# Gates and u of a spatial-gating layer by seven block products instead of eight, multiplied onto y in place

## The chip, the cores and the metric

One core of one Trainium2 chip runs the kernel. Every time is the device time of one execution in microseconds (us). TensorE (PE) multiplies; it has a queue of its own for loading weight blocks (PEld). VectorE (DVE) and ScalarE (ACT) do the elementwise work, GpSimd (POOL) and SyncE (SP) issue transfers here.

## What is computed

Two layers on x of 512 rows by 1024 columns, in float32: differential attention, then causal spatial gating. The change is in the second layer, of branch width 2048:

```python
proj = h @ w_in                                  # 512x1024 @ 1024x6144
u = proj[..., :BRANCH]
v = rms_norm(proj[..., BRANCH:2 * BRANCH], v_gain)
gate = proj[..., 2 * BRANCH:]
y = jnp.einsum('gts,bcsgd->bctgd', w, v) + b_s   # w: causal 128x128 per group of 128 channels
return u * y * jax.nn.silu(gate)
```

The result goes through an output projection of 2048x1024, a residual sum and a last norm.

## The kernel before

**Exact products from two parts.** Each float32 operand is split into a high part (ACT rounds it to fp32r) and a low part (DVE subtracts), and a product takes three matmuls: high x high, high x low, low x high. h lies transposed in `hT[0]` and `hT[1]`, as 8 blocks of 128 channels by 512 rows.

**Weights by chunks.** `chunks` lists loads of 1 MB each. `Chunk(i)` (L140) splits chunk i in four pieces with `split` (L122: ACT L137, DVE L138), loads the two after it, and its `tick` splits the next chunk's pieces while PE works. Raw halves rotate through three buffers (`wraw`), split ones through three pairs (`wsp`).

**v by seven block products.** v's weights (1024x2048) are taken as two blocks of 1024x1024. `Quads` (L308) loads the four quarters a, b, c, d of a block (512x512 each), combines them (subtractions on DVE, L334; additions by an accumulating DMA on POOL's queue, L339), and splits each of seven forms (L347, L348). `sides` (L766) holds the seven matching forms of h: quarters of `hT`, and the sums s1 to s4 in a pool of their own, filled by `raw_sums` (L737). `product_n` (L768) gives one product: 2 row blocks x 4 channel blocks x 3 matmuls of 512 columns, 24 in all, with a block of h as the weights. The loop at L806 runs 2 blocks x 7 products. Beside product i it splits the form of product i + 2 (`beside`, `quads.work`). Two pairs of banks, px and py, collect the products; after some of them a state is kept on ACT (`keep`, L792) or added to a kept one on DVE (`plus`, L800), so that seven products give all four quarters of the block. v stands transposed in `yT`, in channel groups; `total` (L795) gathers its squares.

**Norm, then gates and u by chunks.** L858 to L862 make v's scale and multiply `yT` by it. w_s is loaded by POOL (L867), masked (L868) and transposed on PE (L889, L890). Then for each of 8 chunk pairs `gate(c)` projects two groups of gate channels with `proj_t` (L252: per group 8 channel blocks x 3 matmuls, a 128x128 block of weights against 512 columns of h) and applies Silu on ACT (L882). The loop at L891 mixes a group of v with w_s (L897, four matmuls into psy), adds gain and bias (L901), multiplies by the gate (L904), projects u (psu) and multiplies by it (L907), in place in `yT`.

**Output.** `out_half` (L278) splits `yT` into `hT`'s place and multiplies by the output's weights.

**What sets the order.** The program is written as one sequence. A planner (the tile framework) then orders each engine's instructions: among those that are ready by its own estimate of times, the earliest in the program goes first. It inserts the waits, too. Each engine then runs its list strictly in order, so that a wait holds up what stands behind it. `tc.issue_after` ties an instruction behind another by hand. Transfers of weights are issued on SyncE's queue, the accumulating ones and those of w_s and the bias on POOL's.

## Time and profile before

| what | value |
|---|---|
| median of 3 runs | 939.6 us (939.35 to 939.84) |
| profiled execution, its own time | 937.86 us |
| span of its instructions | 936.2 us |
| mean granted clock of TensorE | 0.998 of 2.4 GHz |

The span is the time from the first to the last instruction of the profiled execution; the rest of its own time lies around it. An engine's busy time is the time in which at least one of its instructions runs. A matmul's duration includes its way through the array, and matmuls overlap, so the distance between the starts of two neighbours is what one costs when they follow each other. A view of groups gives, per line of code and shape, the count, busy time, mean time of one, and the idle time ahead of it with what ended it.

### The profile page before, as it was taken

What the parts mean: (1) busy time and instruction counts of PE and PEld (TensorE: products, weight loads), DVE (VectorE), ACT (ScalarE), POOL (GpSimd) and SP (SyncE); (2) the same over time, 40 slices, a digit from 0 to 9 for tenths busy, and PEclk for the clock granted to TensorE, in tenths of its full rate; (3) what the DMA queues carried; (4) which work ended last, traced back from release to release, by engine and by line L of the source; (5) the groups of instructions that cost most, each with busy time, mean ns of one, the idle gap of its engine ahead of it and who ended that gap; (6) DMA issues with size and microseconds to landing.
All of it is one profiled execution on the core that took longest, in us unless ns stands there. A gap on an engine that the chain in (4) does not pass through costs nothing.

```text
span 936.2 us, 12287 instructions
## 1 busy us (share of the span) xinstructions
PE 918.1 (98%) x4553; PEld 751.9 (80%) x4553; DVE 539.4 (58%) x1329; ACT 414.5 (44%) x981; POOL 16.7 (2%) x29
## 2 busy tenths in 40 slices
PE   7999999999999999999999999999999999999996
PEld 5878887878787878787778887788888888888884
DVE  7532225757675667576877739955633333365634
ACT  6332334545454545555656426856322222233432
POOL 0000000000000000000000000001000000000000
PEclk9999999999999999999999999999999999999999
DMA  7432223222222223131214624545422222232202
GB/s 247 145 115 90 90 90 100 71 84 84 80 81 77 87 72 95 63 102 57 67 50 161 207 62 78 176 90 168 125 90 89 88 86 88 90 101 97 91 16 90
DMA packets 64795, 92.29 MB, mean 99 GB/s; under 512 B 3597, under 2 KB 44606, under 8 KB 64096
## 3 DMA queue, kind: packets, MB, share of 16 engines
q1 hardware_dynamic: 61408, 79.70, 26.5%
q0 software_dynamic: 2272, 10.49, 4.4%
q10 hardware_dynamic: 1056, 1.32, 0.5%
q8 instruction: 36, 0.59, 0.2%
q14 instruction: 23, 0.19, 0.1%
HBM read 85.17 MB, written 2.14 MB: 93 GB/s over the span
## 4 chain that ended last, share of the span: by engine, by line
PE 86%; DVE 8%; ACT 3%; DMA 1%; issue 1%; SPq 0%; ACTq 0%
PE psv L426 10%; PE psqk L256 6%; PE psqk L258 6%; PE psqk L257 6%; PE acc L293 5%; PE acc L291 5%; PE acc L292 5%; PE pss L565 3%; PE psg L256 3%; PE psu L257 3%; PE psu L256 3%; PE psu L258 3%; PE psg L257 3%; PE psgt L257 3%; PE psgt L256 3%; PE psg L258 3%
## 5 line engine op out<-in xcount | busy, mean ns | idle before, releaser
L138 DVE TENSOR_TENSOR lo<-raw,hi 128x512 fp32r<-128x512 f32 x256 | 165.1, 684 | 165.7 <-ACT hi L137 165.7
L137 ACT CAST hi<-raw 128x512 fp32r<-128x512 f32 x256 | 144.9, 618 | 208.5 <-PE psu L257 72.4
L256 PE MATMUL psqk<-hT,hi 128*128 128x512 f32 x256 | 104.3, 407 | 0.0
L578 ACT ACTIVATE e<-e,nm 128x384 f32<-128x384 f32 (+3 forms) x128 | 70.6, 553 | 67.5 <-DVE nm L575 67.5
L258 PE MATMUL psqk<-hT,lo 128*128 128x512 f32 x256 | 100.2, 391 | 0.0
L257 PE MATMUL psqk<-hT,hi 128*128 128x512 f32 x256 | 99.9, 390 | 0.0
L291 PE MATMUL acc<-hi,hT 128*128 128x512 f32 x224 | 88.1, 393 | 0.0
L293 PE MATMUL acc<-hi,hT 128*128 128x512 f32 x224 | 87.4, 390 | 0.0
L292 PE MATMUL acc<-lo,hT 128*128 128x512 f32 x224 | 87.3, 390 | 0.0
L426 PE MATMUL psv<-hi,hT 128*128 128x512 f32 x256 | 86.8, 405 | 0.5 <-ACT hT L247 0.5
L575 DVE CUSTOM_DVE_ANT_0 e<-pss,bias 128x384 f32<-128x384 f32 (+3 forms) x128 | 55.6, 485 | 17.6 <-PE pss L565 17.4
L426 PEld LDWEIGHTS psv<-hi,hT 128*128 128x128 f32 x256 | 48.6, 190 | 13.9 <-issue 2.2
L256 PEld LDWEIGHTS psqk<-hT,hi 128*128 128x128 f32 x256 | 48.1, 188 | 12.9 <-issue 2.6
L258 PEld LDWEIGHTS psqk<-hT,lo 128*128 128x128 f32 x256 | 48.1, 188 | 10.5
L257 PEld LDWEIGHTS psqk<-hT,hi 128*128 128x128 f32 x256 | 48.2, 188 | 8.9
L285 ACT CAST hT<-yT 128x512 fp32r<-128x512 f32 x56 | 33.5, 622 | 45.0 <-PE acc L292 32.5
L286 DVE TENSOR_TENSOR hT<-yT,hT 128x512 fp32r<-128x512 f32 x56 | 37.5, 688 | 26.8 <-PE acc L292 26.0
L256 PE MATMUL psu<-hT,hi 128*128 128x512 f32 x128 | 51.2, 400 | 0.0
L426 PE MATMUL psv<-lo,hT 128*128 128x512 f32 x128 | 50.4, 395 | 0.0
L256 PE MATMUL psg<-hT,hi 128*128 128x512 f32 x128 | 49.9, 390 | 0.0
L257 PE MATMUL psu<-hT,hi 128*128 128x512 f32 x128 | 49.9, 390 | 0.0
L258 PE MATMUL psu<-hT,lo 128*128 128x512 f32 x128 | 49.9, 390 | 0.0
(187 smaller groups left out, 1739.5 us busy)
## 6 DMA issues: line engine op xcount, KB each, us to landing
raw<-in_attn_w_in SPq DMA_DIRECT2D x62, 512.0 KB, 3.9
raw<-in_sgu_w_in SPq DMA_DIRECT2D x32, 512.0 KB, 4.5
raw<-in_attn_w_out SPq DMA_DIRECT2D x16, 512.0 KB, 3.4
quarter<-in_sgu_w_in SPq DMA_DIRECT2D x16, 512.0 KB, 4.9
raw<-in_sgu_w_out SPq DMA_DIRECT2D x16, 512.0 KB, 3.9
bias<-tb POOLq DMA_DIRECT2D x16, 256.0 KB, 3.6
quarter<-quarter POOLq DMA_DIRECT2D x4, 1024.0 KB, 7.3
xr<-in_x SPq DMA_DIRECT2D x4, 512.0 KB, 4.7
```

Source lines behind the costliest of these rows:

```text
L137: nc.scalar.copy(hi[:, sl], raw)
L138: nc.vector.tensor_tensor(lo[:, sl], raw, hi[:, sl].bitcast(F32), ALU.subtract)
L256: nc.tensor.matmul(ps, lhsT=w.hi[:, k, cs], rhs=hT[0][:, k, :], start=(k == 0), stop=False)
L257: nc.tensor.matmul(ps, lhsT=w.hi[:, k, cs], rhs=hT[1][:, k, :], start=False, stop=False)
L258: nc.tensor.matmul(ps, lhsT=w.lo[:, k, cs], rhs=hT[0][:, k, :], start=False, stop=(k == KD - 1))
L286: nc.vector.tensor_tensor(yl[:, i], yT[:, k, :], yh[:, i].bitcast(F32), ALU.subtract)
L291: nc.tensor.matmul(acc[b], lhsT=yh[:, j, bs], rhs=w.hi[:, j, :], start=(k == 0), stop=False)
L292: nc.tensor.matmul(acc[b], lhsT=yh[:, j, bs], rhs=w.lo[:, j, :], start=False, stop=False)
L293: nc.tensor.matmul(acc[b], lhsT=yl[:, j, bs], rhs=w.hi[:, j, :], start=False, stop=(k == KB - 1))
L426: nc.tensor.matmul(ps[b], lhsT=hT[a][:, k, bs], rhs=m[:, j, :], start=(k == 0 and a == 0 and m is w[half].hi), stop=(k == KD - 1 and a == 1))
L575: nc.vector.tensor_tensor_reduce(out=e[f][:, cs], in0=ps[f][:, cs], in1=hd.bias[:, S - n:S], scale=-1.0, scalar=-NEG, op0=ALU.add, op1=ALU ...
L578: nc.scalar.activation(e[f][:, cs], e[f][:, cs], AF.Exp, scale=-1.0, bias=nm[:, col], accum_out=l[:, col])
```

## The change

The gates and u of the second layer are computed as v is: their weights form four more blocks of 1024x1024, and `quads` now has six (`columns`: two of v, then gates and u of the first 1024 channels, then gates and u of the others). `product_t` gives one product with a 128x128 block of weights against 256 columns of h: 4 x 4 x 3 = 48 matmuls. `hold` keeps a state of px on ACT, `times` adds (DVE), applies Silu for gates (ACT) and multiplies onto `yT` in place (DVE). `mix` is the mixing with w_s; it follows chosen products. The sum s3 takes the place of a quarter of `hT` that no product reads, and that quarter is no longer written. w_s and half of the bias are loaded and masked in v's first block and transposed in its second; the other half of the bias is loaded later. The output's first weights are split beside the last two products.

```diff
--- before.py
+++ after.py
@@ -98,9 +98,6 @@
         for c in range(4):
             chunks.append(wide_src(w_out, c, m * S))
     sgu_at = len(chunks)
-    for base, c in sorted(((base, c) for c in range(NH // 2) for base in (2 * BR, 0)),
-                          key=lambda z: (z[1] - (z[0] > 0), z[0] == 0)):
-        chunks.append(in_src(sgu_w_in, base + c * 2 * P))
     for m in range(2):
         for c in range(4):
             chunks.append(wide_src(sgu_w_out, c, m * S))
@@ -662,10 +659,12 @@
+    columns = [BR, BR + D, 2 * BR, 0, 2 * BR + D, D]
+
     def sgu_quarter(n):
         def of(name):
             r, c = divmod("abcd".index(name), 2)
-            return wide_src(sgu_w_in, r, BR + n * D + c * S)[0]
+            return wide_src(sgu_w_in, r, columns[n] + c * S)[0]
         return of
 
     run(out_half(i0, 0, hT_store, [3], acc, residual(1, 0, acc)))
@@ -677,7 +676,7 @@
         return [yp.tile([P, 4, S], F32R, tag=t, name=t) for t in ("yh", "yl")]
 
     acc = [bank(f"acc{b}") for b in range(NB)]
-    quads = Quads(qp, [sgu_quarter(n) for n in range(BR // D)])
+    quads = Quads(qp, [sgu_quarter(n) for n in range(len(columns))])
     gen = out_half(i0 + 4, 1, lambda c: (hT_store if c < 2 else yp_store)(c), range(4), acc,
                    residual(1, 1, acc))
 
@@ -714,6 +713,9 @@
+    def of_h(q, half):
+        return [h[:, 4 * q:4 * q + 4, half * H:(half + 1) * H] for h in hT]
+
     def part(hi, lo, raw):
         nc.scalar.copy(hi, raw)
         nc.vector.tensor_tensor(lo, raw, hi.bitcast(F32), ALU.subtract)
@@ -732,7 +734,16 @@
     yps.__exit__(None, None, None)
     scope = tc.tile_pool(name="sums", bufs=1)
     sp = scope.__enter__()
-    sums = {n: [sp.tile([P, 4, H], F32R, name=f"{n}{t}") for t in ("h", "l")] for n in ("s1", "s2", "s3", "s4")}
+    sums = {n: [sp.tile([P, 4, H], F32R, name=f"{n}{t}") for t in ("h", "l")] for n in ("s1", "s2", "s4")}
+    sums["s3"] = of_h(0, 1)
+
+
+    wst = sp.tile([P, KB, P], F32, name="wst")
+    bs_bc = sp.tile([P, KB // 2 * P], F32, name="bs_bc")
+
+    def spread_bias(m):
+        src = sgu_b_s.rearrange("o g t -> o (g t)")[:, m * KB // 2 * P:(m + 1) * KB // 2 * P]
+        nc.gpsimd.dma_start(bs_bc, src.broadcast_to([P, KB // 2 * P]))
 
     def raw_sums(b, pq):
         hs = slice(b % 2 * P, (b % 2 + 1) * P)
@@ -755,13 +766,8 @@
         part(*put["s4"])
         yield
         sl = slice(b * P, (b + 1) * P)
-        for q in (1, 0):
-            qs = slice(4 * q, 4 * q + 4)
-            part(hT[0][:, qs, sl], hT[1][:, qs, sl], pq[q])
+        part(hT[0][:, 4:8, sl], hT[1][:, 4:8, sl], pq[1])
         yield
-
-    def of_h(q, half):
-        return [h[:, 4 * q:4 * q + 4, half * H:(half + 1) * H] for h in hT]
 
     sides = [of_h(0, 0), of_h(1, 0), sums["s2"], sums["s3"], sums["s1"], sums["s4"], of_h(1, 1)]
 
@@ -812,11 +818,6 @@
             ps = py if i in (1, 3, 6) else px
             a, w = sides[i], quads.forms[n, i]
             work = quads.work(7 * n + i + 2)
-            if n == BR // D - 1 and i == 5:
-                limit[0] = len(chunks)
-                load(i0)
-            if n == BR // D - 1 and i > 4:
-                work = (split(i0, 2 * (i - 5) + h) for h in range(2))
             units = product_n(ps, a, w, i in (0, 1, 3))
             if n == 0 and i < 2:
                 for u, _ in enumerate(units):
@@ -850,8 +851,17 @@
                     total(*value(n, 1, 0, h))
             if i == 6:
                 plus(n, 0, 1, py)
-    scope.__exit__(None, None, None)
-    quarters.__exit__(None, None, None)
+            if n == 0 and i == 4:
+                nc.gpsimd.dma_start(wst, sgu_w_s[0].rearrange("g t s -> t g s"))
+                spread_bias(0)
+                nc.gpsimd.affine_select(wst, wst, pattern=[[0, KB], [-1, P]], compare_op=ALU.is_ge, fill=0.0, base=0,
+                                        channel_multiplier=1)
+            if n == 1 and 1 <= i < 5:
+                q = i - 1
+                pt = bank("ptw")
+                for j in range(4):
+                    nc.tensor.transpose(pt[:, j * P:(j + 1) * P], wst[:, 4 * q + j, :], ident)
+                nc.vector.tensor_copy(wst[:, 4 * q:4 * q + 4, :], pt.rearrange("p (g t) -> p g t", t=P))
 
     vs = small.tile([P, NB], F32, name="vs")
     vrs = const.tile([P, NB], F32, name="vrs")
@@ -861,54 +871,94 @@
         sl = slice(b * P, (b + 1) * P)
         nc.vector.tensor_scalar(yT[:, :, sl], yT[:, :, sl], vrs[:, b:b + 1], None, ALU.mult)
 
-    scope = tc.tile_pool(name="sgu", bufs=1)
-    sp = scope.__enter__()
-    wsn = sp.tile([P, KB, P], F32, name="wsn")
-    nc.gpsimd.dma_start(wsn, sgu_w_s[0].rearrange("g t s -> t g s"))
-    nc.gpsimd.affine_select(wsn, wsn, pattern=[[0, KB], [-1, P]], compare_op=ALU.is_ge, fill=0.0, base=0,
-                            channel_multiplier=1)
-    bs_bc = sp.tile([P, KB * P], F32, name="bs_bc")
-    nc.gpsimd.dma_start(bs_bc, sgu_b_s.rearrange("o g t -> o (g t)").broadcast_to([P, KB * P]))
-    wst = sp.tile([P, KB, P], F32, name="wst")
-
-    sg = {}
-
-    def gate(c):
-        w = Chunk(i0 + (0 if c == 0 else 2 * c - 1), 16)
-        for j in range(2):
-            ps = bank("psgt")
-            run(proj_t(ps, w, j))
-            sg[2 * c + j] = sp.tile([P, S], F32, name="sg", bufs=5)
-            nc.scalar.activation(sg[2 * c + j], ps, AF.Silu)
-
-    gate(0)
-    gate(1)
-    for q in range(KB // 4):
-        pt = bank("ptw")
-        for j in range(4):
-            nc.tensor.transpose(pt[:, j * P:(j + 1) * P], wsn[:, 4 * q + j, :], ident)
-        nc.vector.tensor_copy(wst[:, 4 * q:4 * q + 4, :], pt.rearrange("p (g t) -> p g t", t=P))
-    for c in range(KB // 2):
-        w = Chunk(i0 + (2 * c + 2 if c < KB // 2 - 1 else 2 * c + 1), 16)
-        for j in range(2):
-            g = 2 * c + j
-            py = bank("psy")
-            for b in range(NB):
-                nc.tensor.matmul(py[:, b * P:(b + 1) * P], lhsT=yT[:, g, b * P:(b + 1) * P], rhs=wst[:, g, :],
-                                 start=True, stop=True)
-            bb = bs_bc[:, g * P:(g + 1) * P].unsqueeze(1).broadcast_to([P, NB, P])
-            yg = yT[:, g, :]
-            nc.vector.scalar_tensor_tensor(yg.rearrange("p (b t) -> p b t", b=NB),
-                                           py.rearrange("p (b t) -> p b t", b=NB), gv[:, g:g + 1], bb,
-                                           ALU.mult, ALU.add)
-            nc.vector.tensor_tensor(yg, yg, sg[g], ALU.mult)
-            ps = bank("psu")
-            run(proj_t(ps, w, j))
-            nc.vector.tensor_tensor(yg, ps, yg, ALU.mult)
-        if c + 2 < KB // 2:
-            gate(c + 2)
-    i0 += 16
+
+    def product_t(ps, a, w, start):
+
+        for f in range(4):
+            for k in range(4):
+                for t, (x, y) in enumerate(((0, 0), (0, 1), (1, 0))):
+                    clear = start and f % 2 == 0 and k == 0 and t == 0
+                    nc.tensor.matmul(ps[f // 2][:, f % 2 * H:(f % 2 + 1) * H], lhsT=w[x][:, k, f * P:(f + 1) * P],
+                                     rhs=a[y][:, k, :], start=clear, stop=(k == 3 and t == 2),
+                                     skip_group_check=not (start and f % 2 == 0))
+                yield
+
+    px, py = [[bank(t) for _ in range(2)] for t in ("px", "py")]
+    psy = [bank("psy") for _ in range(4)]
+
+    def mix(g):
+
+        ps, yg = psy[g % 4], yT[:, g, :].rearrange("p (b t) -> p b t", b=NB)
+        for b in range(NB):
+            nc.tensor.matmul(ps[:, b * P:(b + 1) * P], lhsT=yT[:, g, b * P:(b + 1) * P], rhs=wst[:, g, :],
+                             start=True, stop=True)
+        bb = bs_bc[:, g % 8 * P:(g % 8 + 1) * P].unsqueeze(1).broadcast_to([P, NB, P])
+        nc.vector.scalar_tensor_tensor(yg, ps.rearrange("p (b t) -> p b t", b=NB), gv[:, g:g + 1], bb,
+                                       ALU.mult, ALU.add)
+
+    def temp():
+        return wraw.tile([P, 2, S], F32, tag="raw", name="raw")
+
+    def hold(t, ps):
+        for f in range(2):
+            nc.scalar.copy(t[:, f], ps[f])
+
+    def times(gates, m, c, half, ps, t=None, add=True):
+
+        for f in range(2):
+            g = 8 * m + 4 * c + 2 * f
+            v = ps[f]
+            if add:
+                nc.vector.tensor_tensor(t[:, f], ps[f], t[:, f], ALU.add)
+                v = t[:, f]
+            if gates:
+                nc.scalar.activation(t[:, f], v, AF.Silu)
+                v = t[:, f]
+            y = yT[:, g:g + 2, half * H:(half + 1) * H]
+            nc.vector.tensor_tensor(y, v.rearrange("p (j n) -> p j n", n=H), y, ALU.mult)
+
+    VB = BR // D
+    for m in range(2):
+        for gates in (True, False):
+            n = VB + 2 * m + (not gates)
+            final = m == 1 and not gates
+            t1 = temp()
+            if final:
+                t4, t2 = temp(), temp()
+            for i in range(7):
+                work = quads.work(7 * n + i + 2)
+                if final and i == 5:
+                    limit[0] = len(chunks)
+                    load(i0)
+                if final and i > 4:
+                    work = (split(i0, 2 * (i - 5) + h) for h in range(2))
+                beside(product_t(py if i in (1, 3, 6) else px, sides[i], quads.forms[n, i], i in (0, 1, 3)), work)
+                if m == 0 and gates and i in (2, 3):
+                    for g in range(4 * i - 8, 4 * i - 4):
+                        mix(g)
+                    if i == 3:
+                        spread_bias(1)
+                if m == 0 and not gates and i > 2:
+                    mix(5 + i)
+                if m == 1 and gates and i < 4:
+                    mix(12 + i)
+                if i == 0:
+                    hold(t1, px)
+                if i == (2 if m == 0 and gates else 1):
+                    times(gates, m, 0, 0, py, t1)
+                if i == 2:
+                    t2 = t2 if final else temp()
+                    hold(t2, px)
+                if i == 4:
+                    t4 = t4 if final else temp()
+                    hold(t4, px)
+                    times(gates, m, 1, 1, py, t4)
+                if i == 5:
+                    times(gates, m, 1, 0, px, temp() if gates else None, False)
+                if i == 6:
+                    times(gates, m, 0, 1, py, t2)
     scope.__exit__(None, None, None)
+    quarters.__exit__(None, None, None)
```

## Rows read from the trace of the kernel before

**Rows 1.** The page's engine line: busy us (share of the span) and instructions.
```profile
PE 918.1 (98%) x4553; PEld 751.9 (80%) x4553; DVE 539.4 (58%) x1329; ACT 414.5 (44%) x981; POOL 16.7 (2%) x29
```

**Rows 2.** Windows of three stretches: stretch, length, then as the first row says.
```profile
core 0: us, PE busy (x) PEld busy (x) DVE busy (x) ACT busy (x) POOL busy (x), PEclk, DMA share, GB/s
566.00:611.00 45.00, 43.80 (x198) 34.55 (x197) 42.14 (x64) 32.62 (x56) 0.88 (x1) 1.00 0.40 117
611.00:649.00 38.00, 38.00 (x166) 30.91 (x165) 22.33 (x27) 24.32 (x44) 3.46 (x4) 1.00 0.43 101
649.00:840.00 191.00, 190.85 (x915) 160.39 (x914) 84.19 (x137) 49.96 (x90) 2.00 (x1) 1.00 0.34 104
```

**Rows 3.** Timeline of PE, then of weight loads: start us, us, what, count.
```profile
649.07 0.39 PE L256 MATMUL psgt<-hT,hi 128*128 128x512 f32 x1
...
659.95 0.39 PE L256 MATMUL psgt<-hT,hi 128*128 128x512 f32 x1
...
649.07 0.19 PEld L257 LDWEIGHTS psgt<-hT,hi 128*128 128x128 f32 x1
```

**Rows 4.** Tile views: count, ns min/median/max, first and last start us.
```profile
L256 PE MATMUL psgt<-hT,hi x128: 389/389/389, 649.1 to 813.7; 128*128 128x512 f32 x128
...
L258 PE MATMUL psu<-hT,lo x128: 389/389/397, 674.3 to 839.6; 128*128 128x512 f32 x128
...
L897 PE MATMUL psy<-wst,yT x128: 270/275/348, 672.9 to 834.2; 128*128 128x128 f32 x128
```

**Rows 5.** Timeline: weight loads of the scores, then a burst of mixing matmuls.
```profile
152.69 0.19 PEld L565 LDWEIGHTS pss<-qkl,qkh 64*128 64x128 f32 x2
152.80 0.19 PEld L565 LDWEIGHTS pss<-qkh,qkl 64*128 64x128 f32 x2
...
833.46 1.05 PE L897 MATMUL psy<-wst,yT 128*128 128x128 f32 x8
```

**Rows 6.** Timeline of PE: score matmuls of 384 columns, then of 256.
```profile
152.34 0.34 PE L565 MATMUL pss<-qkl,qkh 64*128 64x384 f32 x2
...
152.69 0.22 PE L565 MATMUL pss<-qkh 64*128 64x128 f32 x2
...
157.34 0.28 PE L565 MATMUL pss<-qkl,qkh 64*128 64x256 f32 x2
...
157.81 0.28 PE L565 MATMUL pss<-qkh,qkl 64*128 64x256 f32 x2
```

**Rows 7.** Groups by form, 560 to 660 us, then 649 to 840 us.
```profile
L348 DVE TENSOR_TENSOR lo<-quarter,hi 128x1024 fp32r<-128x1024 f32 x24 | 28.3, 1218 | 9.1 <-ACT hi L347 9.1
L347 ACT CAST hi<-quarter 128x1024 fp32r<-128x1024 f32 x24 | 24.3, 1050 | 12.5 <-DMA quarter<-quarter 8.8 <-DVE quarter L334 3.0 <-PE py L776 0.6
L792 ACT COPY yT<-px 128x512 f32<-128x512 f32 x16 | 9.2, 586 | 7.4 <-PE px L776 5.6 <-DVE s4l L719 1.8
L800 DVE TENSOR_TENSOR yT<-py,yT 128x512 f32<-128x512 f32 x12 | 8.0, 684 | 3.4 <-ACT yT L792 1.8 <-PE py L776 1.6
...
L901 DVE SCALAR_TENSOR_TENSOR yT<-psy,cols,bs_bc 128x512 f32<-128x512 f32 x16 | 12.0, 747 | 1.6 <-PE psy L897 1.6
...
L882 ACT ACTIVATE sg<-psgt 128x512 f32<-128x512 f32 x16 | 9.5, 595 | 23.9 <-PE psgt L258 23.9
```

**Rows 8.** Timeline of DVE around the norm of v.
```profile
649.27 0.69 DVE L800 TENSOR_TENSOR yT<-py,yT 128x512 f32<-128x512 f32 x1 [0.68 <-PE py L776]
...
657.33 0.69 DVE L138 TENSOR_TENSOR lo<-raw,hi 128x512 fp32r<-128x512 f32 x1 [5.63 <-ACT hi L137]
...
660.18 4.87 DVE L862 TENSOR_SCALAR yT<-yT,vrs 128x2048 f32<-128x2048 f32 x4
```

**Rows 9.** Chain of waits, 574 to 600 us, then timeline of POOL.
```profile
577.57 7.07 DMA quarter<-quarter
...
577.57 0.88 POOL L339 DMA_DIRECT2D quarter<-quarter  x1 [18.14 <-ACT hi L347]
...
644.50 1.20 POOL L867 DMA_DIRECT2D wsn<-in_sgu_w_s  x1 [22.79 <-DMA raw<-in_sgu_w_in]
```

## The prediction

> **What bounds the kernel now.** I read the engine line of the page first, then the windows by stretch, then single matmuls. TensorE (PE) is busy 98% of the span [rows 1], and through the stretch that the change rewrites, 649 to 840 us, it is busy 190.85 of 191.00 us at a granted clock of 1.00, its upper level of 2.4 GHz [rows 2]. VectorE (DVE) works 84.19 us of it and ScalarE (ACT) 49.96 us: both wait for PE. So this stretch lasts as long as its matmuls take to follow each other. A matmul's shown duration (389 ns) is no price, since the next one starts long before it ends; the price is the distance between starts. From 649.07 to 659.95 us 48 matmuls of 512 columns start [rows 3]: 10.88 / 48 = 0.2267 us each. The gates and u have six groups of 128 such matmuls [rows 4], 768 x 0.2267 = 174.1 us. With 128 mixing matmuls (psy) at 0.111 us [rows 5], 14.2 us, and 16 transposes of w_s at about the same, 1.8 us, that makes 190.1 us of the 190.8 us between the first psgt start and the end of the last psu [rows 4]: nothing but PE's own stream is in there.
>
> **What goes, what comes.** Gone are the 768 matmuls: -174.1 us. In their place come 2 halves x (gates, u) x 7 products x 48 = 1344 matmuls, each with a 128x128 weight block and 256 moving columns. In columns that is 1344 x 256 / (768 x 512) = 7/8. The gain stands or falls with the spacing of one 256-column matmul, which the trace does not show with 128 rows. Break-even is 174.1 / 1344 = 0.1295 us.
>
> Three rows bound it. **From below**: a weight load runs during the matmul ahead of it (the load for the second psgt matmul starts at 649.07, as the first starts [rows 3]), and loads that follow each other at once start 0.11 us apart (152.69, 152.80); the mixing burst of eight gives the same, (1.05 - 0.275) / 7 = 0.111 us [rows 5]. So 0.111 us is the floor. **Nearest row**: the attention scores have matmuls of 64 rows x 256 columns, in pairs that run together. Four steps from 157.34 to 157.81 take 0.1175 us each [rows 6]. The same pairs with 384 columns take (152.69 - 152.34) / 2 = 0.175 us [rows 6]. Those two widths give a fixed part of 3 x 0.1175 - 2 x 0.175 = 0.0025 us: nearly all of the time goes with the columns. Halving the full-row matmul in that way gives (0.2267 - 0.0025) / 2 + 0.0025 = 0.1146 us. **From above**: were a column to pass in each cycle of 2.4 GHz, 512 columns would be 0.2133 us; were the remaining 0.0134 us all fixed per matmul, 256 columns would take 0.120 us. I take 0.115 us, the halved row, just over the floor: 1344 x 0.115 = 154.6 us. Ends for the range: 0.111 (149.2 us) and 0.120 (161.3 us).
>
> Of page rules, one gives a lower price: the Trainium skill, "TensorE: Matmul & The Clock Gate", section "Back-to-back issue gap", has N / 2.4 + 2.5 ns as the spacing, which is 215.8 ns at 512 columns where this trace shows 226.7 [rows 3], and 109.2 at 256. By it the new matmuls would take 146.8 us, an estimate under the floor shown above, so I keep the rows.
>
> **Work of the other engines per block of seven products** (7 x 48 x 0.115 = 38.6 us of PE). DVE: 14 low parts at 1.22 us (17.1), 4 subtractions of that size (4.9), 6 additions and 8 multiplications of 128x512 at some 0.69 (9.7) [rows 7]: 31.7 us. ACT: 14 high parts at 1.05 us (14.7), 6 copies at 0.59, and for gates 8 Silu at 0.60: 23 us. Both fit beneath 38.6. Removed from them are 64 pieces of 128x512 each of splitting, 16 Silu and 32 multiplications, which lay beside PE and pay nothing back.
>
> The tight place is the first new block. It inherits the norm of v: the last sum starts 0.2 us after PE's last v product (649.27), reduction and Newton steps follow, then four scalings, 4.87 us [rows 8], 8 us in all, and 8 mixing results at 0.75 us (6.0) [rows 7]. DVE then owes 31.7 + 8 + 6 = 45.7 us beside 38.6 + 8 x 0.45 = 42.2 us of PE. The excess of 3.5 us is covered: two forms are split before the block begins, 11 us ahead; scaling should be over some 11 us after PE's last v product, at the end of the second product, and mixing follows the third (in the trace it ends at 665.05, 16 us after, because a low part ahead of the last Newton steps waited 5.63 us for a load [rows 8]; even that is before the third product's end); and the multiplications that may slip have a block behind them that owes 31.7 + 3 of 40.4 us. If that cover went, PE would wait at the third or fourth product.
>
> Waits inside the new blocks: the same scheme runs in v's second block without any (611 to 649 us: PE busy 38.00 of 38.00) and loses 1.2 us in the first (566 to 611 us, 43.80 of 45.00) [rows 2]. For four blocks 0 to 4.8 us; as they resemble the second block (operands on hand, loads a block ahead) I take 1 us. SyncE's loads keep their bytes and their 32 issues of 512 KB. POOL issues 8 more accumulating DMAs; one takes 7.07 us [rows 9]. A block's first is needed by the seventh product's form, its second (issued in the first product) by the fifth's, which is split two products earlier, during the third: 11 us on.
>
> **What moves.** The 16 transposes go into v's second block, 1.8 us there and 1.8 us less later: 0. Their four copies fit, as DVE is busy 22.33 of 38 us [rows 2]. The w_s load, its masking (POOL's 2.00 us in [rows 2]) and half the bias go from 644.50 us [rows 9] to v's first block. On POOL they may stand ahead of the accumulating DMA of 577.57 us, on which the chain of waits hangs for 7.07 us [rows 9]; behind it wait ACT's high part and s3h, and PE. Before it POOL idles 18.14 us [rows 9], so I take 0; bounds are 0 and 7 us, another transfer of that size ahead. Against that, s3 now lies in rows of h that no product reads, and the gates no longer need those rows: two high and two low parts, about 1.2 us each on ACT and DVE, fall out where DVE is busy 42.14 of 45.00 us [rows 2]; I give nothing for it, up to 1 us. The other half of the bias and the next stage's loads are off the path. In the last block the output's weights are split beside products 6 and 7, and half of h is free for the output's operands after product 4: the output stage starts as it did, 0.
>
> **Sum**: -174.1 + 154.6 + 1 + 0 = -18.5 us. The profiled execution took 937.86 us (span 936.2, 1.7 around it), 1.7 under the median of the three runs, 939.6. It would become 919.4, and the median 939.6 - 18.5 = **921.1 us**. A measurement of this kernel tells 0.2%, about 1.9 us, from no change.
>
> **Rivals.**
> 1. *A fixed cost per matmul* (spacing 0.120): for it, only one width with full rows is shown; against it, the 64-row widths that scale. -174.1 + 161.3 + 1 = -11.8: 927.8 us.
> 2. *The other engines hold PE up*: DVE in the first new block, an accumulating DMA before ACT's high part in each, or the moved loads in v's first block. For it, DVE's 45.7 us of work and the 7.07 us on the chain; against it, v's second block without a wait. At 1.2 us a block and 3 us in v's first: 8 us rather than 1: 928.1 us.
> 3. *Slower: weight loads no longer hidden.* The place is each of the 1344 new matmuls: a load takes 0.111 us of the 0.115, where it had 0.2267. If a full-row load could not run wholly beneath a matmul on the same rows, spacing grows; it decides from 0.1295 us. With half of the load bare, 0.115 + 0.055 = 0.170 us, 1344 of them take 228.5 us: 939.6 + 228.5 - 174.1 + 1 = 995 us. Against it: now the load starts with the matmul ahead and 0.2267 is less than 0.2133 plus a load [rows 3], and the 64-row pairs hide their loads at 0.1175 [rows 6]. For it: those loads fill half of the rows only. The Trainium skill, "TensorE: Matmul & The Clock Gate", section "Part 3: Packing small matmuls — row/col tiling", has weight loads overlap a matmul in flight only where the row groups differ, which is this rival outright; rows 3 contradict it at 512 columns, so it gets little.
> 4. *The change doesn't do what it says*: the planner's order puts products in a row with their forms, so that the saved columns come back as waits; about 939 us.
>
> **Chances.** Forecast (0.111 to 0.1175, waits up to 3 us) 0.62; rival 1 0.19; rival 2 0.12; rival 3 0.05; rival 4 0.02. Faster by over 0.2% are the first three, 0.93; within 0.2% 0.02; slower 0.05. Low end: 0.111 without waits, 24.9 us, about 915. High end: 0.120 with 3 us, 9.8 us, about 930; beyond lie rivals 3, 4 and parts of the first and second, 2 in 10 at most.
>
> **What would show it.** The first starts of two neighbouring 256-column matmuls: 0.115 apart (right), 0.120 (rival 1), over 0.13 (rival 3). PE's count up by 576; the stretch from v's last product to the output some 170 us, with PE busy throughout; low parts of quarters 84 in place of 28. PE idle at the third or fourth product of the first new block, or a longer wait for the quarter's DMA in v's first, would be rival 2. A spacing over 0.12 would make the forecast wrong.

## The result and the profile after

The changed kernel takes 927.8 us (median of 4 runs, 926.35 to 928.58) against 939.5 for the kernel before (4 runs, 939.27 to 939.84): ratio 0.987, 95% interval 0.986 to 0.989. That is 11.7 us faster where 18.5 were forecast; it lies in the range, at the number of the first rival. The profiled execution took 928.58 us, the longest of its four; its span of 926.8 us is 9.4 under that of before.

The page's engine line, which answers to [rows 1]:

```profile
PE 904.7 (98%) x5129; PEld 768.6 (83%) x5129; DVE 598.2 (65%) x1359; ACT 446.1 (48%) x995; POOL 24.9 (3%) x38
```

PE's count is up by 576, as 1344 for 768 must give. Next the windows of v's two blocks and of the new products, for [rows 2]:

```profile
core 0: us, PE busy (x) PEld busy (x) DVE busy (x) ACT busy (x) POOL busy (x), PEclk, DMA share, GB/s
566.00:612.00 46.00, 43.19 (x199) 33.93 (x198) 42.86 (x71) 33.31 (x58) 5.03 (x4) 1.00 0.53 152
612.00:656.00 44.00, 42.28 (x192) 34.36 (x191) 29.99 (x32) 23.20 (x39) 1.71 (x2) 1.00 0.53 144
656.00:831.00 175.00, 175.00 (x1476) 174.89 (x1475) 133.73 (x163) 81.56 (x109) 7.78 (x9) 1.00 0.52 139
```

In the new stretch PE is busy all 175 us at the full granted clock, DVE 134 and ACT 82: PE's stream still bounds it, with no waits. PE idles 2.8 us in v's first window and 1.7 in the second, where it lost 1.2 and nothing before [rows 2].

The timeline of PE, for [rows 3]: the first product by `product_t`, one start and one 30 matmuls later, then the last matmul of all.

```profile
656.48 0.40 PE L881 MATMUL px<-hT,hi 128*128 128x256 f32 x2
...
660.08 0.40 PE L881 MATMUL px<-hT,hi 128*128 128x256 f32 x2
...
830.83 0.28 PE L881 MATMUL py<-hT,lo 128*128 128x256 f32 x1
```

3.60 / 30 = 0.120 us each. From the first to the last start of gates and u it is 174.35 us; less the mixing's 14.2, 160.2 / 1344 = 0.119 us on the mean.

**Where the 9.4 us of the profiled pair come from.** Gates and u, first to last start: 190.5 before, 174.35 after, -16.2. v, from its first product (566.39 before, 568.36 after) to the first of gates: 82.68 before, 88.12 after, +5.4, of which 1.8 are the moved transposes. Ahead of v, where nothing was changed, +2.0, over half of it within the first 12 us of the kernel. The output, -0.6. Forecast were -20.3 (-174.1 - 1.8 + 154.6 + 1), +1.8, 0 and 0. So two things are to be explained: 4 us in the new products, and 3.6 in v. The 2.0 us ahead of v are no part of the change: in the profiles of the runs below v starts 0 to 1.8 us later than before the change.

v's lost time shows in the timelines. First block, POOL, DVE and PE in turn:

```profile
576.18 2.41 POOL L857 TENSOR_SCALAR_AFFINE_SELECT wst<-wst 128x2048 f32<-128x2048 f32 x1 [5.29 <-DMA wst<-in_sgu_w_s]
581.36 0.89 POOL L336 DMA_DIRECT2D quarter<-quarter  x1 [2.77 <-DVE lo L345]
...
576.64 4.16 DVE L345 TENSOR_TENSOR lo<-quarter,hi 128x1024 fp32r<-128x1024 f32 x2
...
572.75 0.50 PE L780 MATMUL px<-hi,hT 128*128 128x512 f32 x1 [0.63 <-ACT hT L711]
...
584.99 0.50 PE L782 MATMUL px<-hi,s2l 128*128 128x512 f32 x1 [0.95 <-DVE s2l L721]
...
602.93 0.50 PE L780 MATMUL px<-hi,s4h 128*128 128x512 f32 x1 [0.28 <-ACT yT L798]
```

Two low parts that take 2.35 us elsewhere take 4.16 here, and they began while POOL masked w_s: DVE's first ended some 3.0 us after its start, not 1.2, and 1.1 us after the mask's end. What stands behind on DVE, s2's low part among it, keeps PE waiting. From the start at 572.75 to that of s4h it is 30.18 us; the same two starts of before are 28.40 apart.

Second block: POOL's and SP's queues, ACT, PE, then pieces of the chain of waits (start, us, what).

```profile
623.50 0.85 POOL L336 DMA_DIRECT2D quarter<-quarter  x1 [7.04 <-DMA quarter<-quarter]
...
623.67 21.22 SPq L326 DMA_DIRECT2D quarter<-in_sgu_w_in  x8
...
634.19 1.05 ACT L344 CAST hi<-quarter 128x1024 fp32r<-128x1024 f32 x1 [9.13 <-DMA quarter<-quarter]
...
648.16 0.50 PE L780 MATMUL px<-hi,s4h 128*128 128x512 f32 x1 [1.72 <-ACT yT L798]
```

```profile
623.50 10.61 DMA quarter<-quarter
...
641.13 3.79 DMA quarter<-in_sgu_w_in
645.05 1.23 DVE quarter L331
646.28 0.61 DVE yT L806
647.63 0.48 ACT yT L798
```

The accumulating DMA takes 10.61 us where one took 7.07 [rows 9]; ACT waits 9.13 us for it. The work behind it is late, then DVE's subtraction for the next block (b - d, which needs that block's quarters) waits for a load, with the addition and ACT's copy of px behind it, and PE stops 1.7 us in the middle of the sixth product.

### The profile page after: what moved, and what is told of

It reads as the page before. It is cut to its first block, busy times and chain, and to the rows that moved or that the text cites. A ratio compares the mean times of both kernels' runs of the same rounds, so it can differ in the third digit from the quotient of the medians.

```text
span 926.8 us, 13474 instructions
## 1 busy us (share of the span) xinstructions
PE 904.7 (98%) x5129; PEld 768.6 (83%) x5129; DVE 598.2 (65%) x1359; ACT 446.1 (48%) x995; POOL 24.9 (3%) x38
## 3 DMA queue, kind: packets, MB, share of 16 engines
HBM read 85.17 MB, written 2.14 MB: 94 GB/s over the span
## 4 chain that ended last, share of the span: by engine, by line
PE 81%; DVE 10%; DMA 4%; ACT 3%; issue 1%; SPq 0%; ACTq 0%; POOLq 0%; DVEq 0%
PE psv L423 10%; PE px L881 10%; PE py L881 7%; PE psqk L253 6%; PE psqk L255 6%; PE psqk L254 6%; PE acc L289 5%; PE acc L288 5%; PE acc L290 5%; PE pss L562 3%; PE psg L253 3%; PE psg L254 3%; PE psg L255 3%; PE po L600 3%; DMA quarter<-quarter 3%; DVE lo L345 2%
## 5 line engine op out<-in xcount | busy, mean ns | idle before, releaser
L135 DVE TENSOR_TENSOR lo<-raw,hi 128x512 fp32r<-128x512 f32 x192 | 124.4, 687 | 104.4 <-ACT hi L134 104.2
L134 ACT CAST hi<-raw 128x512 fp32r<-128x512 f32 x192 | 109.4, 619 | 104.2 <-PE psqk L254 44.2
L345 DVE TENSOR_TENSOR lo<-quarter,hi 128x1024 fp32r<-128x1024 f32 x84 | 102.2, 1242 | 44.4 <-ACT hi L344 39.8
L344 ACT CAST hi<-quarter 128x1024 fp32r<-128x1024 f32 x84 | 85.9, 1047 | 93.0 <-DMA quarter<-quarter 36.6
L881 PE MATMUL py<-hT,hi 128*128 128x256 f32 x384 | 69.9, 284 | 0.0
L881 PEld LDWEIGHTS py<-hT,hi 128*128 128x128 f32 x384 | 59.8, 192 | 0.0
L255 PEld LDWEIGHTS psqk<-hT,lo 128*128 128x128 f32 x256 | 48.0, 188 | 10.5
L881 PE MATMUL py<-hT,lo 128*128 128x256 f32 x192 | 54.3, 283 | 0.0
```

The source lines that it names most:

```text
L134: nc.scalar.copy(hi[:, sl], raw)
L135: nc.vector.tensor_tensor(lo[:, sl], raw, hi[:, sl].bitcast(F32), ALU.subtract)
L255: nc.tensor.matmul(ps, lhsT=w.lo[:, k, cs], rhs=hT[0][:, k, :], start=False, stop=(k == KD - 1))
L344: nc.scalar.copy(hi[:, sl], raw[:, sl])
L345: nc.vector.tensor_tensor(lo[:, sl], raw[:, sl], hi[:, sl].bitcast(F32), ALU.subtract)
L881: nc.tensor.matmul(ps[f // 2][:, f % 2 * H:(f % 2 + 1) * H], lhsT=w[x][:, k, f * P:(f + 1) * P], rhs=a[y][:, k, :], start=clear, stop=(k = ...
```

## The experiments

Ratios are against the kernel before, run on the same chip. "The row block to s4h" is the stretch of 30.18 us above; "the pause" is PE's in the sixth product of v's second block.

**1. The changed kernel again.** No edit.

> The changed kernel itself, timed beside the three variants of it. Both theories: 927.8 us, in single runs 926.3 to 928.6. The matmul stretch from its first to its last 256-column matmul lasts 174.5 us again and v's two blocks 90 us.

Measured: 925.98 us (925.15 to 926.93) against 938.33, ratio 0.987 (0.985 to 0.989), 1.8 under the 927.8 expected. v takes 86.05 us, 2.1 less than in the first profile and not the 90 expected; gates and u take 174.35 to the hundredth. The first block is as slow as in the first profile (34.56 us from v's first product to s4h, 34.57 there, 32.78 before the change); the pause is gone. POOL, SP and ACT at the same place:

```profile
622.25 0.85 POOL L336 DMA_DIRECT2D quarter<-quarter  x1 [6.69 <-DMA quarter<-quarter]
...
622.77 18.74 SPq L326 DMA_DIRECT2D quarter<-in_sgu_w_in  x8
...
630.82 1.05 ACT L344 CAST hi<-quarter 128x1024 fp32r<-128x1024 f32 x1 [6.66 <-DMA quarter<-quarter]
```

ACT starts 8.6 us after the issue, not 10.7. The load of the next block is issued 0.52 us behind the accumulating DMA, not 0.17.

**2. The mask out of the first block.** w_s is masked on POOL only behind the second accumulating DMA of v's second block, the transposes two products later (`last_add` is that DMA, noted where it is issued):

```diff
-                nc.gpsimd.affine_select(wst, wst, pattern=[[0, KB], [-1, P]], compare_op=ALU.is_ge, fill=0.0, base=0,
-                                        channel_multiplier=1)
-            if n == 1 and 1 <= i < 5:
-                q = i - 1
+            if n == 1 and i == 1:
+                with tc.issue_after(quads.last_add.ins):
+                    nc.gpsimd.affine_select(wst, wst, pattern=[[0, KB], [-1, P]], compare_op=ALU.is_ge, fill=0.0,
+                                            base=0, channel_multiplier=1)
+            if n == 1 and 3 <= i < 7:
+                q = i - 3
```

> The masking of w_s on POOL is moved out of v's first block to its second, behind the second accumulating DMA there; its transposes follow two products later. Theory (while POOL masks, DVE's SBUF work runs at about half speed: the pair of low parts took 4.16 us in place of 2.35, and the accumulating DMA, s2 and s3 came later by as much): the pair is back at 2.35 us, v's first block loses 1.9 us less, 925.9 us. Rival (the load of w_s and the bias holds up the accumulating DMA): nothing changes, 927.8 us.

Measured: 926.39 us against 938.33, ratio 0.987 (0.986 to 0.989), so no gain over the 925.98 of the changed kernel beside it. The first block does what was expected: the row block to s4h takes 28.31 us, 1.87 less than 30.18, and DVE's pair its usual time:

```profile
576.20 2.35 DVE L345 TENSOR_TENSOR lo<-quarter,hi 128x1024 fp32r<-128x1024 f32 x2
```

But the second block gave it back: v takes 87.11 us in all. Its accumulating DMA is long in this program, and PE waits 0.65 us ahead of the fifth product and has the pause:

```profile
621.16 10.54 DMA quarter<-quarter
...
645.84 0.50 PE L780 MATMUL px<-hi,s4h 128*128 128x512 f32 x1 [1.81 <-ACT yT L798]
```

**3 and 4. The subtraction one product later in the text** (`if i == 0` to `if i == (1 if n else 0)` ahead of b - d), alone and with the late mask.

> For all blocks but the first the subtraction b-d is done beside one product later, so that in v's second block DVE doesn't wait for the next block's quarter ahead of the additions of the fourth and fifth product. Theory (that wait put the addition, ACT's copy behind it and the sixth product late): the gap of 2.1 us ahead of the sixth product of v's second block closes, 925.8 us. Rival (the accumulating DMA of 10.6 us is the cause, and ACT's order holds the copy anyway): a gap of 1 us or more stays there, 927 to 928 us.

> The two edits together, mask and subtraction. If both waits are what was named and lie one behind the other, the gains add: 927.8 - 1.9 - 2.0 = 923.9 us. If one of them falls away only for the other to take its place: 925.8 us or more.

Measured against the same 938.33: 925.75 us, ratio 0.987 (0.986 to 0.988), and 927.61 us, 0.989 (0.987 to 0.990). Neither is the experiment it was meant to be: every engine's order, instruction by instruction, is that of the kernel without the edit. The planner left the subtraction where it was. They are repeats: late_sub of the changed kernel (no pause), the run `both` of late_mask (the pause again).

**5. The matmul's spacing by itself.** A kernel that computes nothing of the reference: streams of 96 matmuls in fp32r from on-chip operands, by columns and by size of the weight block, then DVE subtractions beside a mask on POOL.

> A kernel of its own that computes nothing of the reference: streams of 96 matmuls of the same three terms, one stream per width, with ACT, DVE and transfers at rest; then DVE subtractions of 128x1024 alone and beside a mask of 128x2048 on POOL. Fixed part per matmul (rival 1): starts 0.227 us apart at 512 columns, 0.173 at 384, 0.120 at 256, with weights of 64 columns (half the load) still 0.120, and at 128 columns the loads' 0.109 to 0.112. Time goes with the columns (the forecast's step): 0.171 at 384, 0.1146 at 256. Weight load nearly bare: 0.120 at 256 with full weights, 0.115 or less with weights of 64 columns. DVE: 1.2 us alone; beside the mask about 2.1 us by the theory on POOL, 1.2 us by its rival.

The views by line for PE (count, ns min/median/max, first and last start): one of the three terms at 512 columns, of the other streams the first term and the last.

```profile
L62 PE MATMUL p<-hl,wh x32: 389/389/389, 40.2 to 61.3; 128*128 128x512 f32 x32
...
L65 PE MATMUL p<-hh,wh x32: 333/334/346, 61.7 to 77.9; 128*128 128x384 f32 x32
...
L65 PE MATMUL p<-hh,wl x32: 334/334/342, 62.1 to 78.2; 128*128 128x384 f32 x32
...
L68 PE MATMUL p<-hh,wh x32: 278/283/283, 78.4 to 89.5; 128*128 128x256 f32 x32
...
L68 PE MATMUL p<-hh,wl x32: 280/283/283, 78.6 to 89.8; 128*128 128x256 f32 x32
...
L74 PE MATMUL p<-hh,wh x32: 224/273/277, 101.4 to 111.7; 128*128 128x128 f32 x32
...
L74 PE MATMUL p<-hh,wl x32: 273/274/277, 101.6 to 112.0; 128*128 128x128 f32 x32
...
L77 PE MATMUL h<-hh,wh x32: 276/276/280, 112.1 to 122.6; 128*64 128x256 f32 x32
...
L77 PE MATMUL h<-hh,wl x32: 276/276/277, 112.3 to 122.9; 128*64 128x256 f32 x32
...
L80 PE MATMUL r<-hh,wh x32: 280/280/384, 123.1 to 134.3; 64*128 64x256 f32 x32
...
L80 PE MATMUL r<-hh,wl x32: 276/280/280, 123.4 to 134.6; 64*128 64x256 f32 x32
```

First to last start over 95: 384 columns 0.1736 us; 256 columns (89.8 - 78.4) / 95 = 0.120; 128 columns 0.111; weight blocks of 64 columns 0.1135; of 64 rows 0.121, with one late start at its head, 0.120 without it. At 512 columns one term gives (61.3 - 40.2) / 93 = 0.227, the whole stream 0.2267. So 512 to 256 columns lie on one line, 0.4167 ns per column and 0.0133 us fixed per matmul. With 64 columns of weights, timed at 256 columns only, the part beyond the columns is 0.007 us; with 64 rows it stays 0.0133. Rival 1's number (0.120 with 64 weight columns as well) fell, so the fixed part goes with the columns of the weight block. Whether it is the load of that block or the part of the array that it fills isn't shown: every matmul in these programs has a load of its own. A wait for the load's end doesn't show: in the trace of before, a load's record ends 0.04 us before the next 512-column matmul starts. The numbers foreseen for a load nearly bare (0.120, and 0.115 or less) were met, but a load that is partly bare at 256 columns doesn't explain the same 0.0133 at 384 and 512.

POOL, then DVE in the last part:

```profile
27.78 5.40 POOL L96 TENSOR_SCALAR_AFFINE_SELECT mask<-mask 128x2048 f32<-128x2048 f32 x1 [25.20 <-DVE mask L95]
...
27.96 1.22 DVE L100 TENSOR_TENSOR e<-raw 128x1024 f32<-128x1024 f32 x1
...
29.43 1.21 DVE L100 TENSOR_TENSOR e<-raw 128x1024 f32<-128x1024 f32 x1
30.56 0.75 DVE L107 COPY y<-xr 128x512 f32<-128x512 f32 x2
```

Here DVE keeps its 1.22 us, the rival's number and not the theory's 2.1, but the mask is stretched to 5.40 (2.00 in [rows 2]): it ends at 33.18, 1.87 after the last of the six DVE instructions that follow each other from 27.62 on. In the changed kernel DVE was stretched by 1.8 and the mask by 0.4. One of the two waits for the other.

**6. The fixed part in the kernel itself.** The kernel before, with each matmul of the gates and u cut into two of 256 columns with the same weights: the same products, 768 more matmuls.

```diff
+                for h in range(2):
+                    hs = slice(h * (S // 2), (h + 1) * (S // 2))
+                    nc.tensor.matmul(ps[:, hs], lhsT=m[:, k, cs], rhs=hT[a][:, k, hs],
+                                     start=(k == 0 and t == 0 and h == 0), stop=(k == KD - 1 and t == 2),
+                                     skip_group_check=(h == 1))
```

> The kernel before the change, with each 512-column matmul of gates and u cut into two of 256, so 1536 matmuls for 768 and no other edit. Fixed part per matmul of 0.0133 us: 768 more of them cost 10.2 us, 949.7 us, with starts 0.120 us apart. Time goes with the columns, fixed part 0.0025 us: 1.9 us, 941.4 us, starts 0.1146 us apart.

Measured: 949.14 us against 938.95, ratio 1.011 (1.009 to 1.013): +10.2 us, 768 x 0.0133. Its timeline has the starts 0.120 us apart (six steps here), PE is busy throughout, and gates and u take 200.4 us for 190.5:

```profile
702.98 0.64 PE L269 MATMUL psu<-hT,hi 128*128 128x256 f32 x4
...
703.70 0.52 PE L269 MATMUL psu<-hT,hi 128*128 128x256 f32 x3
```

The fixed part is what the change pays 576 times over.

**7 and 8. The load of the next block's a one product later in the text**, alone and with the late mask.

> The changed kernel, but from the second block on the load of the next block's quarter a is issued one product later, with that of b. Theory (the second accumulating DMA of v's second block starts within 0.2 to 0.6 us of that load; where the load falls too close behind it the transfer takes 10.6 us in place of some 7, and PE waits 2.1 us ahead of the sixth product): the transfer stays at 7.5 us or less, no gap there in any profile, and the time is that of the executions without the gap, ratio to before 0.986, with a smaller spread. Rival (the long transfer comes from something else): the gap can still be there, ratio 0.987.

> The late mask and the late load together. Theory (the late mask does save 1.9 us in v's first block, and gives it back because everything then stands closer to the load): first block 1.9 us shorter, no gap of 2 us in the second, 1.9 us under the changed kernel, ratio to before 0.985, and faster than both kernels. Rival (what is saved in the first block is waited out at the next transfer whatever the load does): ratio 0.987, with a wait of 1.5 us or more in v's second block.

Measured against 938.9: 925.8 us, ratio 0.987 (0.985 to 0.988), and 927.51, 0.988 (0.986 to 0.989). These too are repeats: every engine's order is unchanged, and the load is still issued right behind the accumulating DMA. With the earlier runs they make a table of seven executions of the accumulating DMA in v's second block:

| program | load issued after it, us | ACT starts after it, us | pause, us | v, us |
|---|---|---|---|---|
| changed kernel, first profile | 0.17 | 10.7 | 1.72 | 88.12 |
| after_again, late_sub, late_load | 0.50 to 0.52 | 8.6 | none | 86.05 to 86.12 |
| late_mask, both, mask_load | 0.20 to 0.27 | 10.6 to 10.7 | 1.81, 1.75, 2.14 | 87.11, 87.05, 88.98 |

The packet records show the difference. In the first profile the load's packets begin 1.2 us after the accumulating DMA's issue and have the DMA engines (0.9 of their time), and the accumulating DMA's own begin only after 3.6 us; in after_again these begin after 1.4 us, ahead of the load's (2.2), and have 0.9 of the engines, the load 0.1 to 0.2. The other executions of each group agree within 0.2 us.

One cost more shows in mask_load: from 646.5 us, behind its pause of 2.14 us, to 649.9 the granted clock is 0.50, the lower level of 1.2 GHz, and 512-column matmuls start some 0.43 us apart. Its v is 1.9 us longer than in late_mask and both, whose clock stays at 1.00 there; by the starts some 1.5 of it, an estimate, is lost in that stretch.

**9 and 10. The load really moved.** From v's second block on, the next block's a goes into a's own slot, which is free only after the accumulating DMA, and b is tied behind it; then the late mask as well.

```diff
-            if i == 3:
+            if i == 3 and not n:
                 self.load(n + 1, "a", s["b"])
             if i == 4:
-                self.load(n + 1, "b", s["a"])
+                if not n:
+                    self.load(n + 1, "b", s["a"])
+                elif n + 1 < len(self.src):
+                    self.load(n + 1, "a", s["a"])
+                    with tc.issue_after(self.last_load.ins):
+                        self.load(n + 1, "b", s["b"])
```

> The changed kernel with the loads of the next block, from v's second block on, put behind the accumulating DMA: the next block's a goes into a's own slot, which comes free only with the split of the fifth form (that form needs the accumulated a), and b follows it on SyncE's queue. Before this edit a's load goes into b's slot and is issued 0.2 us (the profiled changed kernel, late_mask with the load edit) to 0.5 us (after_again) behind the accumulating DMA. Theory (the long accumulating DMA of v's second block, 10.6 us, is that load's bytes going ahead of its own): no load is issued within 3 us of v's second accumulating DMA, this DMA takes 7.5 us or less, and no idle time of PE over 0.3 us is left in v's second block; the time is then that of the best runs of the changed kernel, 924 to 926 us, ratio 0.985 to 0.987. Rival A (the accumulating DMA is long for a reason of its own, its place on POOL's queue or the state of the rings): it takes 10 us or more in this kernel too, and PE idles some 2 us at the sixth product of v's second block. Rival B (the price is only moved): the accumulating DMA is short, but the next block's a now arrives too late for its first form, so that ACT's first high part waits for it and PE idles at a later block's start or at its seventh product; 1 us or more in any of the blocks, ratio 0.988 or more.

> The same placing of the loads, and w_s masked on POOL only behind v's second accumulating DMA (with the transposes two products later), as in late_mask. If both causes found in v's blocks stand and add up (the mask holding DVE's low part in the first block, 1.9 us; the load ahead of the accumulating DMA in the second, 0 to 2.1 us), v's first block takes 28.3 us from its first product to s4h in place of 30.2, no idle time of PE over 0.3 us shows in the second block, and the kernel takes 1.9 us less than tied_load and after_again: 923.5 to 924.5 us, ratio 0.983 to 0.985, faster than both kernels. Rival (the second block gives it back whatever the loads do, since its DVE or ACT is late by itself once the first block is shorter): the first block shortens, but PE idles 1.5 us or more in the second, and the ratio is 0.987 or 0.988 as in late_mask.

Measured: tied_load 926.8 us against 939.19, ratio 0.987 (0.985 to 0.988); mask_tied 925.49, 0.986 (0.984 to 0.987), each slower than its theory's 924 to 926 and 923.5 to 924.5. The theory's first half holds: with the load 10.9 us behind it, the accumulating DMA takes 6.89 and 6.90 us. The second does not: the load, now late, keeps DVE's subtraction waiting, and tied_load's v, 86.71 us, is no shorter than after_again's. Pieces of the chain and DVE's timeline, in tied_load:

```profile
623.00 6.89 DMA quarter<-quarter
...
636.92 6.47 DMA quarter<-in_sgu_w_in
...
643.49 1.23 DVE L331 TENSOR_TENSOR quarter<-quarter 128x1024 f32<-128x1024 f32 x1 [3.05 <-DMA quarter<-in_sgu_w_in]
644.63 0.68 DVE L811 TENSOR_TENSOR yT<-py,yT 128x512 f32<-128x512 f32 x1
```

A pause of 0.38 us is left there. mask_tied, which gets to that place earlier, has 1.28:

```profile
642.95 0.50 PE L785 MATMUL px<-hi,s4h 128*128 128x512 f32 x1 [1.28 <-ACT yT L803]
```

Rival B was right that the price is partly moved, and wrong on where: it is b's subtraction, not a's high part.

**11 and 12. The subtraction really moved**, on top of mask_tied: first in the text once more (all_three), then tied on DVE (`last_plus` is the last addition, noted where it is made).

```diff
-                nc.vector.tensor_tensor(self.tiles[n, dst][:, sl], self.tiles[n, x][:, sl],
-                                        self.tiles[n, y][:, sl], ALU.subtract)
+                with tc.issue_after(self.last_plus.ins) if n == 2 else ExitStack():
+                    nc.vector.tensor_tensor(self.tiles[n, dst][:, sl], self.tiles[n, x][:, sl],
+                                            self.tiles[n, y][:, sl], ALU.subtract)
```

> mask_tied with the subtraction b - d of each block after the first done one product later. In mask_tied the accumulating DMA is short (6.90 us), yet PE still idles 1.67 us before the sixth product of v's second block: on DVE the subtraction of the next block waits 3.41 us for b's load, which the edit made late, and the addition that frees px stands behind it. Theory (this subtraction is all that is left): no idle time of PE over 0.5 us in v's second block, v's first block as in mask_tied (28.3 us), the kernel some 1.5 us below mask_tied: 923.5 to 924.5 us, ratio 0.983 to 0.985. Rival (moved once more): the subtraction one product on still waits for b, or DVE's two subtractions in one product hold up a low part, and PE idles 1 us or more at the seventh product or at the first product of the block of gates; 925.5 us or more.

> mask_tied with the subtraction b - d of the first block of gates tied on DVE behind the last addition of the fifth product of v's second block. (Moving it in the program's text alone, as in late_sub, both and all_three, left every engine's order as it was: the planner put it back, so those three repeat after_again, late_mask and mask_tied.) Theory (what idles PE before the sixth product is DVE's order: the subtraction waits 3.4 to 3.9 us for b's load, with the addition, ACT's square and its copy of px behind it): the additions run some 2.5 us earlier, no idle time of PE over 0.5 us in v's second block, v's first block as in mask_tied (28.3 us), 923.5 to 924.5 us, ratio 0.983 to 0.985, below mask_tied by 1 to 1.7 us. Rival (moved once more): the form of b - d, or the low parts behind it, come late, and PE idles 1 us or more at the seventh product or in the first block of gates; 925.5 us or more.

Measured: all_three 925.57 us against 938.65, ratio 0.986 (0.984 to 0.988), with the order of mask_tied again, a repeat (its pause is 1.66 us; the 1.67 that its expectation gives for mask_tied is 1.28 in its trace). tied_sub 923.95 us against 938.7, ratio 0.9845 (0.983 to 0.986). DVE in tied_sub:

```profile
638.04 0.69 DVE L812 TENSOR_TENSOR yT<-py,yT 128x512 f32<-128x512 f32 x1
...
641.26 0.68 DVE L812 TENSOR_TENSOR yT<-py,yT 128x512 f32<-128x512 f32 x1
641.86 2.35 DVE L346 TENSOR_TENSOR lo<-quarter,hi 128x1024 fp32r<-128x1024 f32 x2
644.13 3.49 DVE L332 TENSOR_TENSOR quarter<-quarter 128x1024 f32<-128x1024 f32 x3
```

The additions no longer stand behind the subtraction, PE has no pause, the row block to s4h takes 28.3 us, and v 84.15 us: before's 82.68 and 1.5 for transposes. Gates and u take 174.4 us as in every other version. This is the fastest version here, some 2 us under the changed kernel's three repeats (925.75 to 925.98). Those ran on other chips, so the two are compared only through the kernel before, where their intervals overlap (0.983 to 0.986 here, 0.985 to 0.989 there): the gain shows in the traces, v being 1.9 us shorter than in after_again, and isn't settled by the times.

## Why the prediction was right and wrong

**The mechanism was right.** PE's stream bounds the stretch before and after; 7/8 of the columns in 1344 matmuls is faster; the loads stay hidden, so rival 3 did not come; DVE and ACT fit beneath PE, and neither the tight first block of gates nor an accumulating DMA in the new blocks holds PE up. The price of 1 us for waits there was 1 us too much. (The rows of before give 190.9 us for the stretch that the prediction puts at 190.8; nothing hangs on it.)

**The step that failed is the term 1344 x 0.115.** It measured 0.119 to 0.120, so 160.2 us rather than 154.6: 5.6 of the 6.8 us missed. The prediction halved the full-row matmul with the fixed part of the 64-row score pairs, 0.0025 us, and kept the remainder over the columns, 0.0134, only as the upper end. Runs 5 and 6 show that the remainder is the fixed part: 0.0133 us per matmul with a weight block of 128 columns, +10.2 us for 768 more. What makes it is open. Two things were wrong with the pairs. The 0.0025 was the difference of 3 x 0.1175 and 2 x 0.175, each from two starts given to 0.01 us: their last digit alone moves it by more than 0.01 either way, four times its size; and the 384-column pairs of that trace that don't wait step by 0.168 to 0.178. And the height was no reason for a smaller constant: matmuls on 64 rows, one at a time, take 0.120 too. The row for the upper end was of the new matmul's own shape, only wider; with hindsight it should have carried the sum, and rival 1 the forecast.

Of the page rule weighed there: the Trainium skill, "TensorE: Matmul & The Clock Gate", section "Back-to-back issue gap", gives the constant of 2.5 ns for the isolated gap between matmuls. It does not agree with any width measured in these streams of a load and a matmul each: the constant is 13.3 ns with weights of 128 columns and 7 with 64. The prediction was right to leave it, and came back to as small a constant by way of the pairs.

**v's blocks were priced at nothing beyond the transposes and cost 1.6 to 3.6 us.** The prediction looked for the price of the moved mask on POOL's queue, ahead of the accumulating DMA, with bounds of 0 and 7 us. The mask did delay it, but not by standing ahead of it: it ran 576.18 to 578.59, POOL then idled 2.77 us for DVE's low part, and the low part was late because DVE waited for the mask (1.87 us back when the mask is moved, run 2). The Trainium skill, "SBUF — State Buffer", section "Who interferes with whom", has a DVE instruction with two inputs in SBUF (the on-chip memory in which these tiles lie) contend with a GpSimd one that reads SBUF, over a port pair that is an exclusive lock. Both traces agree: DVE's subtraction took 3.0 us for 1.22 and ended 1.1 us after the mask; the mask took 5.40 us for 2.00 and ended 1.87 us after DVE's stream. Which of the two goes first isn't shown: by its recorded start (27.78) the mask of run 5 came before the two subtractions (27.96, 29.43) that it waited for.

The other 2 us in the first profile, and some 3 in late_mask and both (near 5 in mask_load, with its clock), come from the loads that the change adds for a third block: there they go past v's second accumulating DMA. The prediction took v's second block as running without any wait, and read that from a stretch in which no load is issued within 19 us behind this DMA. That the load's place decides is shown by the seven executions and by runs 9 and 10. That the pause goes through the subtraction on DVE is shown by run 12 for the order of mask_tied; in the first profile the chain of waits has the same steps, and no run tests it there. Why a third of a microsecond decides which of the two goes first was not settled.

**The rivals.** Rival 1 was right in its spacing. That its 927.8 is the measured time to the tenth is luck: it took 1 us for waits in the new blocks, which cost nothing, and nothing for v, which cost 1.6 to 3.6, and the repeats ran some 2 us below it. Rival 2 was right that v's first block would wait, though not for the moved loads, and wrong for the new blocks. With v's waits taken out (run 12) the kernel gains 14.8 us, and the forecast with only its spacing corrected gives 18.5 - 5.6 + 1 = 13.9.

## What to carry to other kernels

When a matmul is cut into narrower ones, count the matmuls and not only the columns: two widths of the same shape give a line, and its constant is paid for each matmul. When a stage gets a successor of its own kind, its last block gets the successor's loads: read the price of the steady state, not of a last block. An edit in the program's text is an edit of the kernel only if the engines' order changed; in three of the twelve runs here the subtraction did not move, and in two more the load stayed where it was, which their timelines show.

## What was not expected of the hardware

A matmul in fp32r with a weight block of 128 columns costs 13.3 ns beyond its moving columns, the same at 256, 384 and 512 of them (run 5); 7 ns with half the weight block's columns, timed at 256, and no less with half its rows. The second accumulating DMA of v's second block, 1 MB, takes 6.9 to 7.0 us with no load issued within 10 us behind it (runs 9, 10 and 12), some 8.5 with a load issued 0.5 us behind it (runs 1, 3 and 7), and 10.5 to 10.6 with the same load issued 0.17 to 0.27 us behind it (the first profile and runs 2, 4 and 8); the load's packets then go first.
